# Token-major sums for the output projection and the second MLP matrix, gates as broadcast rows

## The chip, the cores and the metric

The kernel runs on one core of a Trainium2 chip. The metric is the device time of one execution in microseconds (us). TensorE (PE) multiplies, VectorE (DVE), ScalarE (ACT) and GpSimd (POOL) do the elementwise work, and SyncE (SP) issues all DMAs from one queue, in order.

## The reference, cut to what matters

Two layers act on 512 tokens of width 1024: 256 context tokens (`z`) and 256 latent tokens (`x`). Layer 1, the last, keeps the latent tokens alone behind its mixers.

```python
for l in range(DEPTH):                    # DEPTH = 2
    y = merged @ w_out                    # 1024 x 1024, end of the token mixers
    x = post_norm(x, mx[2] * y, ln1_g, ln1_b)
    m = square(relu(modulate(x, mx[3], mx[4]) @ w_mlp1)) @ w_mlp2   # 1024 -> 4096 -> 1024
    x = post_norm(x, mx[5] * m, ln2_g, ln2_b)
def post_norm(r, u, g, b): return layernorm(DN_ALPHA * r + u) * g + b
```

The same holds for `z` with its own gates `mz`. A gate has one value for each of the 1024 features, and one set for each half of the tokens.

## The kernel before, in words

All products are made in float32r, three matmuls for one: `W` loads a block of weights (512 KB, tile `raw`, three buffers), and `wsplit` splits it in four parts into `wh` (a cast on ACT, L191) and `wl` (the rest, a subtraction on DVE, L121). `mm3` then runs `wh`·`xh`, `wh`·`xl` and `wl`·`xh` for each of eight blocks of 128 input features (L216, L220, L221). A block of weights is 1024 input features by 128 output features, so the sums come out feature-major: 128 features on the partitions, 256 or 512 tokens along the row.

`out_proj` goes through its tokens in halves of 256 (`a`, called pair `pr` in the norms: two tiles `t` of 128 tokens). For each half it runs eight blocks of `w_out`, and ACT scales each sum by its gate column into a tile `mg` (called `uT`). `mlp` goes through the 4096 hidden features in quarters `q`. In a quarter, eight blocks of `w_mlp1` make the hidden tiles (`p`), and eight blocks of `w_mlp2` make partial sums that DVE adds up in eight tiles `mg` (called `acc`). The last quarter runs its `w_mlp2` blocks once for each half of the tokens, and DVE also scales them by the gate.

After every four blocks `done` starts `norm_seg`, which brings them into token-major form: `post_half` transposes four 128 x 128 pieces on PE into a PSUM bank (`gr` or `ch`), DVE adds `ALPHA` times the residual (`b`, L130), and `bn_stats` takes the row statistics. At the end of layer 1 PE does the addition too: it multiplies the residual by `ALPHA` times the identity (`kaid`, L477) and adds four products with the identity (`kmisc`, L479). When both halves of the features are there, `post_norm` normalizes on DVE, stores the result (`xd`), and `ln_T` transposes the next operand `hh`, `hl`.

What order the engines follow is set in two steps: `stream` and `pump` interleave the generators by a modelled clock (`COL`, `MM`), and a scheduler with a priority list then orders each engine's queue. Beside layer 0's output projection and MLP runs `feed` (`ada_sum`), which computes later gate columns on DVE (tiles `v` and `t`) from weights that take the same three `raw` buffers; `ada` does other columns on PE between the two stages. `small`, the mixers and `branch` lie ahead of all this.

Of the kernel before, what the change touches and what calls it, by code (L numbers as in the profile page):

```python
# [16 lines left out]
L = 512  # L17
# [70 lines left out]
class Net:  # L88
# [68 lines left out]
    def consts2(self):  # L157
        nc, K = self.nc, self.K
        mb = self.T("kmiscb", (128, 3, 128), BF16)
        nc.sync.dma_start(mb, K['miscb'])  # L160
        self.identb = mb[:, 0, :]
        self.negm = [mb[:, 1, :], mb[:, 2, :]]
        mk = self.T("kmmask", (128, 6, 128), BF16)
        nc.sync.dma_start(mk, K['mmask'])
        self.mmask = mk
        self.aident = self.T("kaid", (128, 128))
        self.ts(self.aident, self.ident, ALPHA)
        zrow = self.T("p", (128, 512))
        nc.gpsimd.memset(zrow, 0.0)
        self.imgs = []  # L170
        for j in range(2):
            im = self.dr.tile([4, 129, 128], F32, name=f"img{j}", tag=f"img{j}", bufs=1)
            nc.sync.dma_start(im[:, 0:128, :].rearrange("u p i -> p u i"), zrow.rearrange("p (u i) -> p u i", u=4))
            self.imgs.append(im)
        self.img_n = 0
# [280 lines left out]
                    self.stt(hl[k][:, c], ps[:, kk, :], s, tm, op0=ALU.mult, op1=ALU.subtract)  # L456
            yield 2 * self.MM, 0.3

    def post_begin(self, resid, g, b, tiles):
        nc = self.nc  # L460
        self.gbt = []
        for a in (g, b):
            t = self.T("b", (128, 1024))
            nc.sync.dma_start(t, a.partition_broadcast(128))
            self.gbt.append(t)
        self.res = {t: resid(t) for t in tiles}
        self.pn = {}

    def post_half(self, uT, t, hf, last):

        rh = self.res[t][:, hf * 512:(hf + 1) * 512]
        if not hf:
            self.pn[t] = [], self.T("pst", (128, 2, 6), bufs=4)
        pss, st = self.pn[t]
        ps = self.PS("gr" if t % 2 else "ch")
        if last:
            self.nc.tensor.matmul(ps, self.aident, rh, start=True, stop=False, skip_group_check=True)  # L477
            for k in range(4):
                self.nc.tensor.matmul(ps[:, k * 128:(k + 1) * 128], uT[hf * 4 + k][:, t * 128:(t + 1) * 128],  # L479
                                      self.ident, start=False, stop=(k == 3), skip_group_check=True)  # L480
        else:
            for k in range(4):
                self.tp(ps[:, k * 128:(k + 1) * 128], uT[hf * 4 + k][:, t * 128:(t + 1) * 128])
            self.stt(rh, rh, ALPHA, ps)
            ps = rh
        self.nc.vector.bn_stats(st[:, hf, :], ps)
        pss.append(ps)

    def post_norm(self, ts, out, last=False):

# [32 lines left out]
                self.tt(sm[t][:, 2:3], sm[t][:, 0:1], rs2[t])  # L523
                self.act(r, r, AF.Identity, scale=rs2[t], bias=sm[t][:, 2:3])

    def norm_seg(self, uT, pr, hf, out, last=False):

        for t in (2 * pr, 2 * pr + 1):
            self.post_half(uT, t, hf, last)
            yield (8 if last else 2) * self.MM, 0.5  # L530
        if hf:
            self.post_norm((2 * pr, 2 * pr + 1), out, last)
            if not last:
                yield 0.0, self.D_LN
                yield from self.ln_T(self.res, pr)


    def small_cols(self, l):
# [718 lines left out]
    def seg(mc, f, a):  # L1257

        w = 1 - a // 256
        return mc[:, f, w:w + 1]  # L1260

    def out_proj(self, l, done):
        t0 = self.t0
        mh, ml = [], []
        for k in range(8):
            hi = self.T("p", dt=F32R)
            lo = self.T("p", dt=F32R)
            self.act(hi[:, t0:], self.mg[k], AF.Copy, scale=0.5)
            self.stt(lo[:, t0:], self.mg[k], 0.5, hi[:, t0:].bitcast(F32), op0=ALU.mult, op1=ALU.subtract)
            mh.append(hi)  # L1270
            ml.append(lo)
        uT = []
        for a in range(t0, L, 256):
            for f in range(8):
                ps = yield from self.projg(self.I['w_out'][l][:, f * 128:(f + 1) * 128], (mh, ml), a, a + 256)
                if a == t0:
                    uT.append(self.T("mg"))
                self.act(uT[f][:, a:a + 256], ps, AF.Identity, scale=self.seg(self.modc[l, 2], f, a))
                if f % 4 == 3:
                    done(a // 256, f // 4, uT)  # L1280

    def mlp(self, l, begin, done):
        t0 = self.t0
        acc = [None] * 8
        for q in range(4):
            ah, al = [], []
            for j in range(8):
                c0 = q * 1024 + j * 128
                ps = yield from self.projg(self.I['w_mlp1'][l][:, c0:c0 + 128], self.h, t0)
                r = self.T("s1")  # L1290
                self.act(r[:, t0:], ps, AF.Relu)
                self.tt(r[:, t0:], r[:, t0:], r[:, t0:])
                hi = self.T("p", dt=F32R)
                lo = self.T("p", dt=F32R)
                self.nc.scalar.copy(hi[:, t0:], r[:, t0:])
                self.tt(lo[:, t0:], r[:, t0:], hi[:, t0:].bitcast(F32), op=ALU.subtract)
                ah.append(hi)
                al.append(lo)
            wp = lambda f: self.I['w_mlp2'][l][q * 1024:(q + 1) * 1024, f * 128:(f + 1) * 128]
            for f in range(8 if q < 3 else 0):  # L1300
                ps = yield from self.projg(wp(f), (ah, al), t0)
                if q == 0:
                    acc[f] = self.T("mg")
                    self.nc.scalar.copy(acc[f][:, t0:], ps)
                else:
                    self.tt(acc[f][:, t0:], ps, acc[f][:, t0:], op=ALU.add)
        begin()
        for a in range(t0, L, 256):
            for f in range(8):
                ps = yield from self.projg(wp(f), (ah, al), a, a + 256)  # L1310
                v = acc[f][:, a:a + 256]
                self.tt(v, ps, v, op=ALU.add)
                self.ts(v, v, self.seg(self.modc[l, 5], f, a))
                if f % 4 == 3:
                    done(a // 256, f // 4, acc)


    def run(self):
# [27 lines left out]
        for l in range(DEPTH):  # L1346
            last = l == DEPTH - 1
            segs = [1] if last else [0, 1]
            tiles = [t for pr in segs for t in (2 * pr, 2 * pr + 1)]
            self.t0 = 256 if last else 0  # L1350
            self.delays = self.DELAYS[l]
            self.early = 3
            sm = self.start(self.small(l, self.small_proj(l)), 1.0)
            self.mg = [None] * 8
            self.yd = {(b, k): self.dr.tile([128, 512], F32, name=f"yd{l}_{b}_{k}", tag=f"yd{b}_{k}", bufs=1)
                       for b in range(3) for k in range(8)}
            self.mixers(l, sm)
            self.drain(self.bg)
            self.post_begin(spilled(2 * l - 1) if l else load, I['ln1_g'][l], I['ln1_b'][l], tiles)
# [3 lines left out]
            self.stream(self.out_proj(l, lambda pr, hf, uT: self.start(self.norm_seg(uT, pr, hf, xd[2 * l]), 0.5)))  # L1363
# [9 lines left out]
            def begin():  # L1373
                if not last:
                    self.drain(self.bg)
                    self.ln_begin(l + 1, 0, 1)
                self.post_begin(spilled(2 * l), I['ln2_g'][l], I['ln2_b'][l], tiles)

            def done(pr, hf, acc):
                self.start(self.norm_seg(acc, pr, hf, self.out[0] if last else xd[2 * l + 1], last), 0.5)  # L1380
            self.stream(self.mlp(l, begin, done))
# [77 lines left out]
```

## Time and profile before

| | us |
|---|---|
| median of 3 runs | 2586.37 |
| lowest and highest run | 2582.62, 2587.11 |
| the profiled execution, its own time | 2590.78 |
| its span in the trace | 2589.0 |
| TensorE busy in it | 2504.6 |

The profiled execution is 4.4 us above the median of the runs. Times inside the trace count from the start of the span. Layer 0's output projection lies at about 1102 to 1166, its MLP from there to 1566, layer 1's output projection at 2333 to 2370, and its MLP from 2390 to the end.

### The profile page before, as it was taken

Reading aid. Unit: us, or ns where it says so; the run is one execution under the profiler, and the core shown is the slowest. Engines: PE = TensorE matmul, PEld = TensorE weight load, DVE = VectorE, ACT = ScalarE, POOL = GpSimd, SP = SyncE. Lnnn points to the kernel's source line nnn. Section 1 sums busy time; section 2 is a strip of 40 time slices with the busy share of each in tenths; the row PEclk is TensorE's granted clock in tenths of the full one; section 3 lists DMA queues with packets and bytes.
Section 4 is the critical chain, followed back from the end, with each engine's and each line's share of the span. In section 5 each row is a group of like instructions: output and inputs, shape, how many; then the busy total and the mean of one; then the engine's idle time right before and its main releaser. Section 6 shows DMA issues by size and latency. Waiting matters only on the chain.

```text
span 2589.0 us, 42418 instructions
## 1 busy us (share of the span) xinstructions
PE 2504.6 (97%) x15225; PEld 2153.7 (83%) x15225; DVE 1808.8 (70%) x4779; ACT 1223.0 (47%) x3608; POOL 179.3 (7%) x334
## 2 busy tenths in 40 slices
PE   7999999999999999989999998899999999999998
PEld 3788888888887888887888886788888888997998
DVE  4967767676678565687556477787777777776766
ACT  3544544554454233355333245455545555555653
POOL 1010010010110000000000001001101101000000
PEclk9999999999999999999999999899999999999999
DMA  7323323312325555466455444433343334676664
GB/s 233 94 83 91 103 78 91 95 54 75 93 62 172 158 156 166 129 190 211 143 166 153 125 139 118 115 106 107 84 122 93 84 94 119 190 213 201 199 189 128
DMA packets 538022, 337.91 MB, mean 131 GB/s; under 512 B 46816, under 2 KB 502098, under 8 KB 537810
## 3 DMA queue, kind: packets, MB, share of 16 engines
q1 hardware_dynamic: 537810, 335.19, 44.7%
q8 instruction: 120, 1.97, 0.3%
q14 instruction: 92, 0.75, 0.1%
HBM read 314.17 MB, written 20.97 MB: 129 GB/s over the span
## 4 chain that ended last, share of the span: by engine, by line
PE 78%; DVE 10%; DMA 5%; ACT 3%; issue 2%; POOL 1%; SPq 0%; DVEq 0%; ACTq 0%; POOLq 0%
PE psmm L216 19%; PE psmm L220 19%; PE psmm L221 18%; PE psmm L136 6%; PE psch L136 5%; PE pstr L136 4%; PE psgr L136 2%; DVE wl L121 2%; DVE p L130 2%; PE pstr L133 2%; PE psgr L1202 1%; DVE b L130 1%; DMA my<-img 1%; ACT wh L191 1%; DMA raw<-in_w_mlp_dram 1%
## 5 line engine op out<-in xcount | busy, mean ns | idle before, releaser
L191 ACT CAST wh<-raw 128x256 fp32r<-128x256 f32 x1736 | 609.6, 405 | 785.5 <-PE psmm L220 550.3
L121 DVE TENSOR_TENSOR wl<-raw,wh 128x256 fp32r<-128x256 f32 x1736 | 682.0, 429 | 221.4 <-ACT wh L191 218.4
L216 PE MATMUL psmm<-hh,wh 128*128 128x512 f32 (+1 forms) x2088 | 763.2, 366 | 11.3 <-ACT wh L191 5.2
L220 PE MATMUL psmm<-hl,wh 128*128 128x512 f32 (+1 forms) x2088 | 732.2, 351 | 1.6 <-POOL hl L121 1.6
L221 PE MATMUL psmm<-hh,wl 128*128 128x512 f32 (+1 forms) x2088 | 728.7, 350 | 3.4 <-DVE wl L121 3.4
L216 PEld LDWEIGHTS psmm<-hh,wh 128*128 128x128 f32 x2088 | 397.5, 191 | 62.3 <-ACT wh L191 7.5
L221 PEld LDWEIGHTS psmm<-hh,wl 128*128 128x128 f32 x2088 | 397.0, 190 | 57.6 <-DVE wl L121 5.5
L220 PEld LDWEIGHTS psmm<-hl,wh 128*128 128x128 f32 x2088 | 397.2, 190 | 48.0 <-POOL hl L121 2.8
L216 PE MATMUL psmm<-p,wh 128*128 128x256 f32 (+1 forms) x1152 | 374.8, 326 | 2.1 <-DVE mg L121 1.9
L221 PE MATMUL psmm<-p,wl 128*128 128x256 f32 (+1 forms) x1152 | 369.2, 321 | 4.7 <-DVE wl L121 4.6
L220 PE MATMUL psmm<-p,wh 128*128 128x256 f32 (+1 forms) x1152 | 367.9, 320 | 1.3 <-DVE p L130 1.1
L221 PEld LDWEIGHTS psmm<-p,wl 128*128 128x128 f32 x1152 | 218.1, 189 | 22.4 <-DVE wl L121 6.3
L216 PEld LDWEIGHTS psmm<-p,wh 128*128 128x128 f32 x1152 | 218.2, 190 | 17.4 <-ACT sm L116 1.5
L220 PEld LDWEIGHTS psmm<-p,wh 128*128 128x128 f32 x1152 | 218.2, 189 | 16.7 <-DVE p L130 1.6
L136 PE MATMUL psmm<-wh,hh 128*128 128x256 f32 x512 | 143.6, 280 | 0.0
L130 DVE SCALAR_TENSOR_TENSOR p<-ci,cw,p 128x512 f32<-128x512 f32 (+1 forms) x192 | 137.6, 721 | 8.3 <-ACT p L116 8.1
L136 PE MATMUL psmm<-wl,hh 128*128 128x256 f32 x512 | 143.4, 280 | 0.0
L136 PE MATMUL psmm<-wh,hl 128*128 128x256 f32 x512 | 143.2, 280 | 0.0
L136 PEld LDWEIGHTS pstr<-v,v 128*128 128x128 f32 x768 | 98.4, 191 | 11.4 <-issue 3.0
L136 PE MATMUL pstr<-v,v 128*128 128x128 f32 x768 | 103.3, 277 | 1.3 <-DVE hrs L125 0.4
L130 DVE SCALAR_TENSOR_TENSOR v<-raw,c,v 128x512 f32<-128x512 f32 x112 | 83.7, 747 | 21.9 <-DMA raw<-in_w_ada_dram 21.2
L136 PEld LDWEIGHTS psmm<-wl,hh 128*128 128x128 f32 x512 | 96.2, 188 | 0.7
(264 smaller groups left out, 3365.1 us busy)
## 6 DMA issues: line engine op xcount, KB each, us to landing
raw<-in_w_in_dram SPq DMA_DIRECT2D x224, 512.0 KB
raw<-in_w_mlp_dram SPq DMA_DIRECT2D x136, 512.0 KB
raw<-in_w_ada_dram SPq DMA_DIRECT2D x80, 512.0 KB
raw<-in_w_branch_dram SPq DMA_DIRECT2D x48, 512.0 KB
raw<-in_w_out_dram SPq DMA_DIRECT2D x24, 512.0 KB
p<-in_w_ada_dram SPq DMA_DIRECT2D x32, 256.0 KB
s<-const_toep_dram SPq DMA_DIRECT2D x40, 192.0 KB
yd<-s SPq DMA_DIRECT2D x24, 256.0 KB
```

What stands on the lines that cost most here:

```text
L121: (eng or self.nc.vector).tensor_tensor(out, a, b, op=op)
L130: self.nc.vector.scalar_tensor_tensor(out, a, s, b, op0=op0, op1=op1)
L133: self.nc.tensor.transpose(out, in_, ident if ident is not None else self.ident)
L136: self.nc.tensor.matmul(out, lhsT, rhs, start=start, stop=stop)
L191: self.nc.scalar.copy(hi, src)
L216: i = self.nc.tensor.matmul(ps, hi[:, k, :], a, start=(k == 0 and clear), stop=False, skip_group_check=not clear)
L220: self.nc.tensor.matmul(ps, hi[:, k, :], b, start=False, stop=False, skip_group_check=not clear)
L221: self.nc.tensor.matmul(ps, lo[:, k, :], a, start=False, stop=(k == 7), skip_group_check=not clear)
L1202: self.nc.tensor.matmul(O[i // 2][:, i % 2, :], W[:, cs(i)], V[:, j, :], start=(j == 0 and i % 2 == 0), stop=(j == (1 if i < 2 else 3)), s ...
```

## The change

`tokproj` swaps the operands: 128 tokens of the activations are the stationary operand, and 512 columns of the weights move. The sums come out token-major (128 tokens by 512 features, one PSUM bank), and no transpose is needed in front of the norm. A block of weights is now 256 input features by 512 output features, again 512 KB, and it is split in two parts. In layer 0 the three first quarters of the MLP keep four banks at once, and their sums are added into `acc` as before, by tile and half of the features. In layer 1 the four banks (`gr` and `ch`) hold the sums over all four quarters.

Since features lie along the row, the gate can't be a column any more. `post_begin` writes the gate columns to DRAM as rows (`gd`) and reads each half back as a row of 512, broadcast over 128 partitions (tiles `my` and `ci`). `post_half` multiplies the sum by it, adds the residual and takes the statistics. In layer 0's last quarter the sums so far are multiplied by the gate and added to the residual while the first MLP matrix runs.

```diff
-    def post_half(self, uT, t, hf, last):
+        self.gr = {}
+        for pr in sorted({t // 2 for t in tiles}):
+            d = self.dr.tile([8, 128], F32, name=f"gd{l}_{sec}_{pr}", tag=f"gd{l}_{sec}_{pr}", bufs=1)
+            nc.sync.dma_start(d.rearrange("k p -> p k"), self.modc[l, sec][:, :, 1 - pr])
+            for hf in range(2):
+                t = self.T("ci" if pr else "my", (128, 512))
+                nc.sync.dma_start(t, d[4 * hf:4 * hf + 4].rearrange("k p -> (k p)").partition_broadcast(128))
+                self.gr[pr, hf] = t
+
+    def post_half(self, ps, t, hf, acc=None):
...
-        ps = self.PS("gr" if t % 2 else "ch")
-        if last:
-            self.nc.tensor.matmul(ps, self.aident, rh, start=True, stop=False, skip_group_check=True)
-            for k in range(4):
-                self.nc.tensor.matmul(ps[:, k * 128:(k + 1) * 128], uT[hf * 4 + k][:, t * 128:(t + 1) * 128],
-                                      self.ident, start=False, stop=(k == 3), skip_group_check=True)
+        tm = self.T("s1")
+        self.tt(tm, ps, self.gr[t // 2, hf])
+        if acc is None:
+            self.stt(rh, rh, ALPHA, tm)
         else:
-            for k in range(4):
-                self.tp(ps[:, k * 128:(k + 1) * 128], uT[hf * 4 + k][:, t * 128:(t + 1) * 128])
-            self.stt(rh, rh, ALPHA, ps)
...
+            self.tt(rh, acc, tm, op=ALU.add)
+    def tokproj(self, ap, xs, order, pss, first=True, last=True):
+        xh, xl = xs
+        n = len(order) // 2
+        for k0 in range(0, 8, 2):
+            hi, lo = self.W(ap[k0 * 128:(k0 + 2) * 128, :], 2)
+            if k0 < 6:
+                todo = [(k, t) for k in range(2) for t in order[n:] + order[:n]]
+            else:
+                todo = [(k, t) for t in order for k in range(2)]
+            for kk, t in todo:
+                k = k0 + kk
+                c = slice(t * 128, t * 128 + 128)
+                self.mm(pss[t], xh[k][:, c], hi[:, kk, :], start=(first and k == 0), stop=False)
+                self.mm(pss[t], xl[k][:, c], hi[:, kk, :], start=False, stop=False)
+                self.mm(pss[t], xh[k][:, c], lo[:, kk, :], start=False, stop=(last and k == 7))
...
-                ps = yield from self.projg(self.I['w_out'][l][:, f * 128:(f + 1) * 128], (mh, ml), a, a + 256)
...
-                self.act(uT[f][:, a:a + 256], ps, AF.Identity, scale=self.seg(self.modc[l, 2], f, a))
+                pss = {t: self.PS("gr" if hf else "mm") for t in ts}
+                yield from self.tokproj(self.I['w_out'][l][:, hf * 512:(hf + 1) * 512], (mh, ml), ts, pss)
+                for t in ts:
+                    self.post_half(pss[t], t, hf)
```

PE's queue at the end of layer 1. Before, these rows follow the last three of 24 matmuls of a block (`psmm`): for each of the two tiles of tokens one product of the residual `b` and four of the sums `mg`.

```order
L216 MATMUL psmm_28105<-p_27792,wh_28095 128x256
L220 MATMUL psmm_28105<-p_27793,wh_28095 128x256
L221 MATMUL psmm_28105<-p_27792,wl_28096 128x256
L477 MATMUL psch_28132<-b_27800,kaid_276 128x512
L479 MATMUL psch_28132<-kmisc_63,mg_26013 128x128
L479 MATMUL psch_28132<-kmisc_63,mg_26052 128x128
L479 MATMUL psch_28132<-kmisc_63,mg_26091 128x128
L479 MATMUL psch_28132<-kmisc_63,mg_26130 128x128
L477 MATMUL psgr_28139<-b_27802,kaid_276 128x512
```

In the change the queue ends with the last block of `w_mlp2` itself, six matmuls for one tile of tokens and six for the other.

```order
L136 MATMUL psch_25058<-wh_26682,p_26482 128x512
L136 MATMUL psch_25058<-wh_26682,p_26483 128x512
L136 MATMUL psch_25058<-wl_26683,p_26482 128x512
L136 MATMUL psch_25058<-wh_26682,p_26526 128x512
L136 MATMUL psch_25058<-wh_26682,p_26527 128x512
L136 MATMUL psch_25058<-wl_26683,p_26526 128x512
L136 MATMUL psch_25059<-wh_26682,p_26482 128x512
L136 MATMUL psch_25059<-wh_26682,p_26483 128x512
L136 MATMUL psch_25059<-wl_26683,p_26482 128x512
```

The products with `kaid` and `kmisc` are gone, and the first tile's bank is complete six matmuls ahead of the second's.

DVE's queue in layer 0's output projection, around the first `post_half` of a pair. Before: `wl` are the splits, `v` and `t` the feed's sums, `b` the residual with a transposed bank added.

```order
L121 TENSOR_TENSOR wl_11014<-raw_11011,wh_11013 128x256 x4
L130 SCALAR_TENSOR_TENSOR v_10857<-raw_11027,c_10_84,v_10857 128x512
L130 SCALAR_TENSOR_TENSOR t_10858<-raw_11027,c_10_84,t_10858 128x512
L130 SCALAR_TENSOR_TENSOR v_10857<-raw_11027,c_10_84,v_10857 128x512
L130 SCALAR_TENSOR_TENSOR b_10780<-b_10780,psch_11035 128x512
L130 SCALAR_TENSOR_TENSOR t_10858<-raw_11027,c_10_84,t_10858 128x512
L486 BN_STATS pst_11034<-b_10780 128x6
L130 SCALAR_TENSOR_TENSOR b_10782<-b_10782,psgr_11049 128x512
L121 TENSOR_TENSOR wl_11075<-raw_11072,wh_11074 128x256
L486 BN_STATS pst_11048<-b_10782 128x6
L121 TENSOR_TENSOR wl_11075<-raw_11072,wh_11074 128x256 x3
```

In the change, at the same place:

```order
L121 TENSOR_TENSOR wl_10962<-raw_10959,wh_10961 128x512 x2
L121 TENSOR_TENSOR s_2085_10948<-psmm_10848,my_10788 128x512
L130 SCALAR_TENSOR_TENSOR v_10864<-raw_10970,c_10_84,v_10864 128x512
L130 SCALAR_TENSOR_TENSOR b_10778<-b_10778,s_2085_10948 128x512
L121 TENSOR_TENSOR s_2087_10953<-psmm_10849,my_10788 128x512
L488 BN_STATS pst_10947<-b_10778 128x6
L130 SCALAR_TENSOR_TENSOR b_10780<-b_10780,s_2087_10953 128x512
L130 SCALAR_TENSOR_TENSOR t_10865<-raw_10970,c_10_84,t_10865 128x512
L488 BN_STATS pst_10952<-b_10780 128x6
L121 TENSOR_TENSOR wl_10986<-raw_10983,wh_10985 128x512 x2
```

Two multiplications by the gate (`s` out of `psmm` and `my`) are new, and both splits of the next block (`wl_10986`) stand behind the whole group.

SP's queue early in layer 0's MLP in the change; ahead of the change the loads of `ada` and `mlp` weights followed one another here.

```order
L341 DMA t_11830<-in_b_ada_dram 4x128
L470 DMA gd_5_0_13721<-mc_5_2069_10861 128x8x1
L470 DMA gd_5_1_13727<-mc_5_2069_10861 128x8x1
L345 DMA raw_11834<-in_w_ada_dram 128x2x512
L473 DMA my_13723<-gd_5_0_13721 128x512
L196 DMA raw_11854<-in_w_mlp_dram 128x8x128
L345 DMA raw_11884<-in_w_ada_dram 128x2x512
L473 DMA my_13725<-gd_5_0_13721 128x512
```

The two writes `gd` wait for the gate columns `mc`, and the reads into `my` for the write; weight loads stand behind each.

## Rows read from the trace of the kernel before

**Rows 1.** The page: busy us of each engine, its share of the span, instructions.
```profile
PE 2504.6 (97%) x15225; PEld 2153.7 (83%) x15225; DVE 1808.8 (70%) x4779; ACT 1223.0 (47%) x3608; POOL 179.3 (7%) x334
```

**Rows 2.** Windows: busy us (instructions) of engines by stretch, clock, DMA share, GB/s.
```profile
1102.00:1166.00 64.00, 56.26 (x434) 52.89 (x433) 57.02 (x123) 33.32 (x88) 6.46 (x9) 0.95 0.63 193
...
1510.00:1566.00 56.00, 52.52 (x431) 50.37 (x429) 48.02 (x124) 28.98 (x77) 7.40 (x8) 1.00 0.51 154
...
2400.00:2576.00 176.00, 175.84 (x1494) 175.15 (x1493) 119.65 (x337) 100.93 (x310) 0.00 (x0) 1.00 0.63 179
```

**Rows 3.** Waits of PE, 1095 to 1170: us in total, times, longest.
```profile
PE psmm L221 <- DVE wl L121: 4.1, 3, 3.1
PE psch L133 <- ACT mg L116: 2.7, 4, 1.4
```

**Rows 4.** Timeline and chain (1170.33): last matmul of a stage, the norm's later steps.
```profile
1165.59 0.28 PE L221 MATMUL psmm<-p,wl 128*128 128x256 f32 x1
...
1170.33 1.33 DVE b L130 x2
...
1565.76 0.28 PE L221 MATMUL psmm<-p,wl 128*128 128x256 f32 x1
...
1570.20 1.41 DVE L130 SCALAR_TENSOR_TENSOR b<-b,sm,b 128x512 f32<-128x512 f32 x2
...
2369.18 0.28 PE L221 MATMUL psmm<-p,wl 128*128 128x256 f32 x1
...
2373.09 1.40 DVE L130 SCALAR_TENSOR_TENSOR b<-b,sm,b 128x512 f32<-128x512 f32 x2
...
2576.20 0.28 PE L221 MATMUL psmm<-p,wl 128*128 128x256 f32 x1
...
2584.22 1.28 DVE L130 SCALAR_TENSOR_TENSOR b<-b,sm,b 128x1024 f32<-128x1024 f32 x1
```

**Rows 5.** Timeline of PE (start, us), layer 1's MLP: 66 matmuls of 256 apart.
```profile
2419.74 0.28 PE L220 MATMUL psmm<-p,wh 128*128 128x256 f32 x1
...
2427.51 0.28 PE L220 MATMUL psmm<-p,wh 128*128 128x256 f32 x1
```

**Rows 6.** Timeline of PE, layer 0's MLP: 30 matmuls of 512 apart.
```profile
1299.62 0.39 PE L221 MATMUL psmm<-hh,wl 128*128 128x512 f32 x1
...
1306.62 0.39 PE L221 MATMUL psmm<-hh,wl 128*128 128x512 f32 x1
```

**Rows 7.** The page's groups: a stationary load (busy us, mean ns).
```profile
L220 PEld LDWEIGHTS psmm<-p,wh 128*128 128x128 f32 x1152 | 218.2, 189 | 16.7 <-DVE p L130 1.6 <-DVE p L121 0.6
```

**Rows 8.** The chain that ended last: transposes in layer 0's last quarter.
```profile
1523.75 0.44 PE psgr L133 x4
```

**Rows 9.** The same chain: additions on PE, end of layer 1.
```profile
2563.23 0.90 PE psch L479 x8
2564.84 0.86 PE psgr L477 x2
```

**Rows 10.** Waits of PE, 1500 to 1570.
```profile
PE psmm L216 <- DVE mg L121: 1.9, 3, 1.2
```

**Rows 11.** The chain: DVE's four splits; two sums, two statistics and their ends.
```profile
1120.37 1.34 DVE wl L121 x4
...
1167.55 1.28 DVE b L130 x2
1168.83 1.20 DVE pst L486 x2
1170.03 0.12 DVE sm L497
...
1170.17 0.15 DVE sm L125
```

**Rows 12.** The chain behind layer 0's output projection.
```profile
1176.10 6.14 DMA xd<-b
```

**Rows 13.** Waits of SP for small writes to DRAM, whole span.
```profile
SPq L831 <- DMA img<-vi: 15.5, 13, 1.9
```

More of the change, by code (lines that the diff above doesn't have):

```diff
@@ L165, in consts2 @@
         self.mmask = mk
-        self.aident = self.T("kaid", (128, 128))
-        self.ts(self.aident, self.ident, ALPHA)
         zrow = self.T("p", (128, 512))
@@ L457, in ln_T, with post_begin @@
             yield 2 * self.MM, 0.3
-    def post_begin(self, resid, g, b, tiles):
+    def post_begin(self, resid, g, b, tiles, l, sec):
         nc = self.nc
@@ L474, in post_half @@
         pss, st = self.pn[t]
-        ps = self.PS("gr" if t % 2 else "ch")
-        if last:
-            self.nc.tensor.matmul(ps, self.aident, rh, start=True, stop=False, skip_group_check=True)
-            for k in range(4):
-                self.nc.tensor.matmul(ps[:, k * 128:(k + 1) * 128], uT[hf * 4 + k][:, t * 128:(t + 1) * 128],
-                                      self.ident, start=False, stop=(k == 3), skip_group_check=True)
-        else:
-            for k in range(4):
-                self.tp(ps[:, k * 128:(k + 1) * 128], uT[hf * 4 + k][:, t * 128:(t + 1) * 128])
-            self.stt(rh, rh, ALPHA, ps)
-            ps = rh
-        self.nc.vector.bn_stats(st[:, hf, :], ps)
-        pss.append(ps)
+        tm = self.T("s1")
+        self.tt(tm, ps, self.gr[t // 2, hf])
+        if acc is None:
+            self.stt(rh, rh, ALPHA, tm)
+        else:
+            self.tt(rh, acc, tm, op=ALU.add)
+        self.nc.vector.bn_stats(st[:, hf, :], rh)
+        pss.append(rh)
     def post_norm(self, ts, out, last=False):
@@ L524, in post_norm, with norm_seg @@
                 self.act(r, r, AF.Identity, scale=rs2[t], bias=sm[t][:, 2:3])
[L526 to L535, printed above, removed]
+    def norm_seg(self, pr, out, last=False):
+        self.post_norm((2 * pr, 2 * pr + 1), out, last)
+        if not last:
+            yield 0.0, self.D_LN
+            yield from self.ln_T(self.res, pr)
     def small_cols(self, l):
@@ L1260, in seg @@
         return mc[:, f, w:w + 1]
+    def tokproj(self, ap, xs, order, pss, first=True, last=True):
[13 more added lines that the diff above has]
+                self.mm(pss[t], xh[k][:, c], lo[:, kk, :], start=False, stop=(last and k == 7))
+                yield 3 * 512 * self.COL
     def out_proj(self, l, done):
@@ L1271, in out_proj, with mlp @@
             ml.append(lo)
-        uT = []
-        for a in range(t0, L, 256):
-            for f in range(8):
-                ps = yield from self.projg(self.I['w_out'][l][:, f * 128:(f + 1) * 128], (mh, ml), a, a + 256)
-                if a == t0:
-                    uT.append(self.T("mg"))
-                self.act(uT[f][:, a:a + 256], ps, AF.Identity, scale=self.seg(self.modc[l, 2], f, a))
-                if f % 4 == 3:
-                    done(a // 256, f // 4, uT)
-    def mlp(self, l, begin, done):
+        for pr in range(t0 // 256, 2):
+            for hf in range(2):
+                ts = [2 * pr, 2 * pr + 1]
+                pss = {t: self.PS("gr" if hf else "mm") for t in ts}
+                yield from self.tokproj(self.I['w_out'][l][:, hf * 512:(hf + 1) * 512], (mh, ml), ts, pss)
+                for t in ts:
+                    self.post_half(pss[t], t, hf)
+                if hf:
+                    done(pr)
+    def mlp(self, l, begin, begin2, done):
         t0 = self.t0
-        acc = [None] * 8
+        acc, sums = {}, {}
+        wp = lambda q, hf: self.I['w_mlp2'][l][q * 1024:(q + 1) * 1024, hf * 512:(hf + 1) * 512]
         for q in range(4):
+            if q == 3:
+                begin()
             ah, al = [], []
@@ L1298, in mlp @@
                 al.append(lo)
[L1299 to L1315, printed above, removed]
+                if q == 3 and not t0:
+                    t, hf = j // 2, j % 2
+                    self.tt(acc[t, hf], acc[t, hf], self.gr[t // 2, hf])
+                    self.stt(acc[t, hf], self.res[t][:, hf * 512:(hf + 1) * 512], ALPHA, acc[t, hf])
@@ new lines, in mlp @@
+            if t0:
+                if q == 3:
+                    begin2()
+                for hf in range(2):
+                    if not q:
+                        sums[hf] = {t: self.PS("ch" if hf else "gr") for t in (2, 3)}
+                    yield from self.tokproj(wp(q, hf), (ah, al), [2, 3], sums[hf], q == 0, q == 3)
+                    if q == 3:
+                        for t in (2, 3):
+                            self.post_half(sums[hf][t], t, hf)
+                continue
+            if q == 3:
+                break
@@ new lines, in mlp @@
+            for hf in range(2):
+                pss = {t: self.PS("mm") for t in (0, 1)}
+                pss.update({t: self.PS("ch" if hf else "gr") for t in (2, 3)})
+                yield from self.tokproj(wp(q, hf), (ah, al), [0, 1, 2, 3], pss)
+                for t in range(4):
+                    if q == 0:
+                        acc[t, hf] = self.T("mg")
+                        self.nc.scalar.copy(acc[t, hf], pss[t])
+                    else:
+                        self.tt(acc[t, hf], pss[t], acc[t, hf], op=ALU.add)
@@ L1318, in run @@
+        if t0:
+            done(1)
+            return
+        begin2()
+        for pr in range(2):
+            for hf in range(2):
+                ts = [2 * pr, 2 * pr + 1]
+                pss = {t: self.PS("gr" if hf else "mm") for t in ts}
+                yield from self.tokproj(wp(3, hf), (ah, al), ts, pss)
+                for t in ts:
+                    self.post_half(pss[t], t, hf, acc[t, hf])
+            done(pr)
     def run(self):
@@ L1358, in run @@
             self.drain(self.bg)
-            self.post_begin(spilled(2 * l - 1) if l else load, I['ln1_g'][l], I['ln1_b'][l], tiles)
+            self.post_begin(spilled(2 * l - 1) if l else load, I['ln1_g'][l], I['ln1_b'][l], tiles, l, 2)
             self.ln_begin(l, 3, 4)
@@ L1362, in run @@
                 self.bg = self.start(self.feed(self.FEED, self.GAP[1]))
-            self.stream(self.out_proj(l, lambda pr, hf, uT: self.start(self.norm_seg(uT, pr, hf, xd[2 * l]), 0.5)))
+            self.stream(self.out_proj(l, lambda pr: self.start(self.norm_seg(pr, xd[2 * l]), 0.5)))
             self.hold = True
@@ L1373, in begin, with begin2 @@
             def begin():
+                self.post_begin(spilled(2 * l), I['ln2_g'][l], I['ln2_b'][l], tiles, l, 5)
+            def begin2():
                 if not last:
@@ L1376, in begin, with done @@
                     self.ln_begin(l + 1, 0, 1)
[L1377 to L1381, printed above, removed]
+            def done(pr):
+                self.start(self.norm_seg(pr, self.out[0] if last else xd[2 * l + 1], last), 0.5)
+            self.stream(self.mlp(l, begin, begin2, done))
             self.drain_all()
```

## The prediction

> **What bounds the kernel now.** I read the page first: TensorE is busy 97% of the span [rows 1], so the first question is whether the change takes work from PE. Then the stages it touches, by windows [rows 2]. Layer 1's MLP (2400 to 2576) is PE and nothing else: 175.84 of 176.00 us busy, DVE 119.65. Layer 0's last quarter and its `w_mlp2` blocks (1510 to 1566) are nearly so, 52.52 of 56.00, with DVE at 48.02. Layer 0's output projection (1102 to 1166) is another case: DVE is busy 57.02 of 64.00 us, PE 56.26, and the granted clock is 0.95. What PE waits for there is DVE's splits, 4.1 us, and ACT's scaled sums, 2.7 us [rows 3]. So what a removed matmul is worth differs: all of it in layer 1's MLP, little in layer 0's output projection. Last I read the joints, where PE has finished a stage and the norm runs on DVE before the next operand exists [rows 4]; there every us counts, whichever engine it is on.
>
> **The products themselves.** 1728 matmuls of 256 columns become 864 of 512: 384 in layer 0's output projection, 384 in its last quarter, 192 in layer 1's output projection, 768 in its MLP. From start to start, 66 matmuls of 256 take 7.77 us, 117.7 ns each [rows 5], and 30 of 512 take 7.00 us, 233.3 each [rows 6]. Two narrow ones cost 235.4, one wide one 233.3, so a pair saves 2.1 ns. In the three stages where PE is the bound that is 672 pairs, **1.4 us**. A stationary load lasts 189 ns [rows 7] and a narrow matmul starts every 117.7, so loads already run beside matmuls and halving their number frees no time. The bounds are 0 and 1.8 (864 pairs).
>
> The Trainium skill (TensorE: Matmul & The Clock Gate, section Back-to-back issue gap) says otherwise: in a stream of load and matmul the spacing is set by both, about 81 ns at 128 columns and 131 at 512. On a straight line between these 256 columns would take 98, and 864 pairs would save 864 x (2 x 98 - 131), about 56 us, an estimate from that page. The rows at 233.3 ns for 512 speak against it.
>
> **Transposes and additions on PE.** Gone are 32 transposes in each stage of layer 0, 16 in layer 1's output projection, and, at the end of layer 1, four additions of the residual with four products each. A transpose is 0.44/4 = 0.11 us [rows 8]; an addition is 0.86, its products 0.90 [rows 9]. The last two tiles of a stage belong to the joint; the others stand in PE's queue among matmuls. Layer 0's MLP: 24 x 0.11 = 2.6. Layer 1's output projection: 8 x 0.11 = 0.9. Layer 1's MLP: 2 x (0.86 + 0.90) = 3.5. Together **7.0 us**. Bounds: 4.4 if layer 0's part hides behind DVE, 7.0.
>
> **A bank that was late.** Before the end of layer 0's MLP PE waits 1.9 us for DVE to empty a bank `mm` [rows 10], as each block of 256 needs one of two. Now `mm` and `gr` alternate by half of the features, and a bank has four blocks, 48 matmuls or 11 us, to be emptied. I count **1.9 us**, bounds 0 and 1.9.
>
> **The joints.** Before, the last matmul ends, DVE or ACT scales the sum, PE transposes, DVE adds and takes statistics, and two operations form (r - mean) x g. From the last matmul's end (start + 0.28) to the end of these two: 1171.66 - 1165.87 = 5.8, 1571.61 - 1566.04 = 5.6, 2374.49 - 2369.46 = 5.0 [rows 4]. Now the first tile's bank is full six matmuls (1.4 us) early, so its gate and addition are done when the second tile ends. Behind that DVE does, in its order: gate 0.64 (half of the pair of 1.28, the nearest row for a 512 operation), statistics 0.60, addition 0.64, 0.12, statistics 0.60, 0.15, the two operations 1.33 [rows 4, 11]: 4.1 us. That saves 1.7, 1.5 and 1.0. At layer 1's end DVE finishes 2585.50 - 2576.48 = 9.0 behind the last matmul; now 4.1 + 0.12 + 1.28 + 0.15 + 1.33 + 1.28 = 8.2, so 0.8. Together **5.0 us**. Bounds: 0.8, if the first three vanish because the chain goes on through the store of the residual, 6.14 us [rows 12], and 5.0.
>
> **Layer 0's output projection.** DVE gets eight gates, 8 x 0.64 = 5.1 us; the splits get 16 x (1.34 - 1.28) = 1.0 cheaper [rows 11]. That is +4.1 on an engine busy 57 of 64 us. Against it stand ACT's wait, 2.7 [rows 3], and the transposes, 24 x 0.11 = 2.6, which PE no longer has. Upward the bound is +4.1. Downward: the 434 matmuls of the window [rows 2] at 117.7 ns are 51 us, so -13. I take **0**, nearer to DVE's row, since DVE is the engine that is full.
>
> **What is hidden.** Six writes of gates and twelve reads join SP's queue. A read waits for its write; such waits are 15.5/13 = 1.2 us, the longest 1.9 [rows 13]. Behind it stand weight loads, and behind these the splits. In layer 0 a block feeds PE for 24 x 0.2333 = 5.6 us and three are loaded ahead, so I count nothing; without that cover it is 6 x 1.9 = 11.4. In layer 0's last quarter DVE prepares `acc` with 16 operations, 10.2 us, while the first matrix keeps PE busy for 8 x 5.6 = 45 us with DVE mostly idle. In layer 1 the sums stay in their banks, which takes some 24 additions from an engine that had room: nothing.
>
> **Sum.** 1.4 + 7.0 + 1.9 + 5.0 + 0 = 15.3. The profiled execution took 2590.8, so 2575.5; it lies 4.4 above the median of 2586.4, which becomes **2571**. About 0.2% (5.2 us) is what a measurement can tell from no change here.
>
> **Rivals.**
> - *The forecast*, 0.60; its own range 2564 to 2578.
> - *Output projection set free*, 0.14: with ACT's scaling and PE's transposes gone, PE no longer waits there, and half of the 13 us comes back: 2571 - 6.5, about 2564. For it: the waits and the clock at 0.95 [rows 2, 3]. Against: DVE's load rises.
> - *Gains absorbed*, 0.13: the first three joints (4.2) are lost to the store, layer 0's transposes (2.6) and the bank's wait (1.9) to DVE, and DVE's 4.1 shows in the output projection. 15.3 - 12.8 = 2.5 is left: 2584, no change.
> - *DVE's queue blocks*, 0.11, the slower side: a gate waits for PE's bank, and the splits of the next block stand behind it. The group is 0.64 x 4 + 0.60 x 2 = 3.8 us, with two feed sums 5.1, and only one block (12 x 0.2333 = 2.8 us) is split ahead in the output projection. Before, a group stood there too, without the gates. If PE loses the whole 5.1 at all eight places in layer 0, that is +41 - 15: 2612. It turns slower than before by 0.2% from 20.5/8 = 2.6 us a place.
> - *Wider is faster*, 0.02: if a wide matmul came at the pace of its load, 189 ns, 864 x (235.4 - 189) = 40 us more would go, some 2531. The rows at 233.3 contradict it. The section of the Trainium skill named above is a rule of this kind.
>
> Faster is the first, second and last: 0.76; same 0.13; slower 0.11. The range reaches from the second case with its bound, 2557, to the third, 2584.
>
> **What would show it.** The 512 matmuls in layer 1's MLP start 233 ns apart. No transposes precede the norms, and PE's wait for `mg` is gone. Behind the last matmul of a stage the two operations end after 4.1 us, and after 8.2 at the end. Layer 0's output projection still takes about 64 us with DVE near 0.9. It is wrong if PE waits longer for splits beside the gates, if weights come late behind the gate rows, or if wide matmuls are slower with weights as the moving operand.

## The result and the profile after: 17 us slower

| | before | after |
|---|---|---|
| median us (5 runs each) | 2585.83 | 2604.82 |
| lowest and highest | 2582.62, 2587.11 | 2596.37, 2611.04 |
| ratio, 95% interval | | 1.0066 [1.0051, 1.0081] |
| the profiled execution: own time, span | 2590.78, 2589.0 | 2604.82, 2603.0 |

The ratio's 0.66% of 2586 is 17 us slower (the two medians lie 19.0 apart), where 15 us faster was forecast. The page after says first that the work did shrink. It shows busy us, share and instructions of each engine, and then the chain that ended last by engine:

```profile
PE 2497.8 (96%) x14241; PEld 2104.8 (81%) x14241; DVE 1797.1 (69%) x4566; ACT 1195.0 (46%) x3384; POOL 180.7 (7%) x334
...
PE 77%; DVE 9%; DMA 7%; ACT 3%; issue 3%; POOL 1%; SPq 0%; DVEq 0%; ACTq 0%; POOLq 0%
```

PE has 984 fewer instructions and 7 us less busy time than in [rows 1], in a span that is 14 us longer. The chain's share of DMA is the new thing. In the chain's pieces (start, us, what) one finds which transfers:

```profile
916.81 11.21 DMA gd<-mc
...
1206.57 11.52 DMA gd<-mc
...
1610.42 9.71 DMA raw<-in_w_in_dram
...
2406.41 13.60 DMA raw<-in_w_mlp_dram
...
2434.59 11.19 PE psgr L136 x48
```

Four places, and each is a write of gate columns or the weight load behind one (the third and fourth write are issued at 1605.7 and 2404.7). The first:

DMA traffic from 914 to 934 in slices of 0.5 us: busy share of the DMA engines in tenths, GB/s, and the packets.

```profile
DMA  9999966487000000454235435232276999896968
GB/s 348 336 365 385 262 176 266 35 24 7 0 0 0 0 0 0 52 73 31 22 29 33 22 13 24 23 29 37 59 72 170 365 395 287 299 242 193 254 217 262
DMA packets 4298, 2.70 MB, mean 135 GB/s; under 512 B 2219, under 2 KB 3247, under 8 KB 4297
```

Two writes of 4 KB are issued at 916.8 and 917.2. Their 4-byte packets are gone by 919. Then nothing at all moves for 3 us, and until 928.5 the queue brings 13 to 73 GB/s instead of some 300. SP waits for the write too, as its next instruction reads it:

```profile
SPq L473 <- DMA gd<-mc: 17.6, 2, 9.4
```

But the load of 512 KB issued ahead of that wait, at 917.9, comes no faster than this either, so it looks as if every transfer were held up; e4, which has no read, parts the two. What that does to the engines is best seen in layer 1's MLP, behind the write at 2404.7. Waits of ACT and of PE from 2395 to 2440 (total us, times, longest):

```profile
ACT wh L189 <- DMA raw<-in_w_mlp_dram: 12.0, 4, 9.6
```
```profile
PE psmm L214 <- ACT s L116: 6.6, 1, 6.6
```

The casts wait for weights, and the matmuls for ACT, because the activation that empties their bank stands behind those casts in ACT's queue. The stage, from its first product to the end of its last, as a window (busy us and counts of PE, PEld, DVE, ACT, POOL, then clock, DMA share, GB/s):

```profile
2398.84:2591.18 192.34, 184.77 (x1159) 165.95 (x1157) 115.66 (x269) 102.94 (x268) 1.58 (x2) 0.97 0.62 176
```

Before, the same stage took 185.9 us:

```profile
2390.56:2576.48 185.92, 185.48 (x1564) 183.67 (x1563) 127.09 (x357) 110.12 (x339) 1.58 (x2) 1.00 0.63 180
```

The other large loss lies ahead of the changed stages: layer 0's first `w_out` load is issued at 1080.51 instead of 1073.05, 7.5 us late, after the stop at 917. In e1, which has no such stop there, it is issued at 1072.99.

```profile
1080.51 0.37 SPq L196 DMA_DIRECT2D raw<-in_w_out_dram  x1
```

### The profile page after: what moved, and what is told of

Its sections match the earlier page's. It is cut to its first block, busy times and chain, and to the rows that moved or that the text cites. A ratio compares the mean times of both kernels' runs of the same rounds, so it can differ in the third digit from the quotient of the medians.

```text
span 2603.0 us, 40009 instructions
## 1 busy us (share of the span) xinstructions
PE 2497.8 (96%) x14241; PEld 2104.8 (81%) x14241; DVE 1797.1 (69%) x4566; ACT 1195.0 (46%) x3384; POOL 180.7 (7%) x334
## 4 chain that ended last, share of the span: by engine, by line
PE 77%; DVE 9%; DMA 7%; ACT 3%; issue 3%; POOL 1%; SPq 0%; DVEq 0%; ACTq 0%; POOLq 0%
PE psmm L214 15%; PE psmm L218 14%; PE psmm L219 14%; PE psmm L136 10%; PE psch L136 8%; PE psgr L136 7%; PE pstr L136 4%; DVE p L130 2%; DVE wl L121 2%; PE pstr L133 2%; DMA raw<-in_w_ada_dram 1%; DMA raw<-in_w_mlp_dram 1%; PE psgr L1200 1%; DMA gd<-mc 1%; ACT wh L189 1%
## 5 line engine op out<-in xcount | busy, mean ns | idle before, releaser
L189 ACT CAST wh<-raw 128x256 fp32r<-128x256 f32 (+1 forms) x1544 | 588.3, 432 | 812.4 <-PE psmm L218 426.7
L121 DVE TENSOR_TENSOR wl<-raw,wh 128x256 fp32r<-128x256 f32 (+1 forms) x1544 | 663.1, 463 | 274.5 <-ACT wh L189 271.7
L214 PE MATMUL psmm<-p,wh 128*128 128x512 f32 (+1 forms) x384 | 134.6, 351 | 3.5 <-DVE s L130 3.5
L218 PE MATMUL psmm<-p,wh 128*128 128x512 f32 (+1 forms) x384 | 131.9, 344 | 1.1 <-DVE p L130 1.1
L219 PE MATMUL psmm<-p,wl 128*128 128x512 f32 (+1 forms) x384 | 131.1, 341 | 0.0
L136 PE MATMUL psgr<-wh,p 128*128 128x512 f32 x384 | 121.8, 401 | 1.4 <-ACT wh L189 1.4
L136 PE MATMUL psmm<-wh,p 128*128 128x512 f32 x352 | 111.3, 399 | 0.5 <-ACT s L116 0.3
L136 PEld LDWEIGHTS psmm<-wh,hh 128*128 128x128 f32 x512 | 96.2, 188 | 0.7
```

The costliest lines, as they stand in the source:

```text
L121: (eng or self.nc.vector).tensor_tensor(out, a, b, op=op)
L136: self.nc.tensor.matmul(out, lhsT, rhs, start=start, stop=stop)
L189: self.nc.scalar.copy(hi, src)
L214: i = self.nc.tensor.matmul(ps, hi[:, k, :], a, start=(k == 0 and clear), stop=False, skip_group_check=not clear)
L218: self.nc.tensor.matmul(ps, hi[:, k, :], b, start=False, stop=False, skip_group_check=not clear)
L219: self.nc.tensor.matmul(ps, lo[:, k, :], a, start=False, stop=(k == 7), skip_group_check=not clear)
```

## The experiments

Three theories. **A**: the write of 4-byte elements stops all transfers. **B**: only SP's order is at fault (a read waits for the write, loads stand behind the read). **C**: the loss is elsewhere, in the gates on DVE or in the order of work. Times are medians; ratios are against the kernel before on the same chip, whose medians were 2587.30 (first four runs), 2585.49 (next four) and 2586.72 (last three).

| run | us | ratio, 95% interval | mean clock of its runs |
|---|---|---|---|
| e1_rows_by_pe | 2581.14 | 0.9981 [0.9972, 0.9989] | 0.988 |
| e2_act_queue | 2606.47 | 1.0079 [1.0066, 1.0092] | 0.983 |
| e3_no_write | 2587.92 | 1.0004 [0.9995, 1.0013] | 0.986 |
| e4_before_plus_write | 2600.88 | 1.0059 [1.0045, 1.0074] | 0.988 |
| e5_ada_behind | 2581.86 | 0.9983 [0.9972, 0.9993] | 0.989 |
| e6_half_elements | 2609.62 | 1.0092 [1.0078, 1.0106] | 0.986 |
| e7_64_byte_elements | 2586.55 | 1.0004 [0.9994, 1.0013] | 0.991 |
| e8_layer1_only | 2581.10 | 0.9986 [0.9975, 0.9997] | 0.991 |
| e9_layer0_only | 2589.72 | 1.0012 [1.0003, 1.0021] | 0.989 |
| e10_old_outproj_l0 | 2586.46 | 0.9995 [0.9986, 1.0004] | 0.989 |
| e12_spread_elements | 2588.05 | 1.0007 [0.9997, 1.0017] | 0.990 |

**e1: the gate rows made on PE, and written as rows.**

```diff
-            nc.sync.dma_start(d.rearrange("k p -> p k"), self.modc[l, sec][:, :, 1 - pr])
+            pg = self.PS("tr")[:8, :128]
+            self.tp(pg, self.modc[l, sec][:, :, 1 - pr])
+            row = self.T("gw", (8, 128))
+            nc.scalar.copy(row, pg)
+            nc.sync.dma_start(d, row)
```

> The gate columns are transposed on PE (six transposes of 128 x 8), copied by ACT and written to DRAM as eight rows of 512 B instead of 1024 elements of 4 B; everything else is as in the change. In the trace of the change nothing moves on the DMA queue for 3 us behind each scattered write, and little for 6 more, at four places. Theory A (the scattered write stops all transfers) and theory B (only SP's order is at fault: a read waits for the write, weight loads stand behind the read) both say that most of the loss goes: 7 us ahead of layer 0's output projection and some 6 to 10 in layer 1's MLP, so about 2583 to 2590. Theory C (the loss is somewhere else: the gates on DVE, the order of `ada` among the matmuls) says 2600 to 2606.

2581.14: C falls, and the change without its scattered write beats the kernel before by 6 us. The write now also stands later in SP's order than in the change, so e1 alone does not part A from B.

**e2: the same writes and reads, issued by ACT.**

```diff
-            nc.sync.dma_start(d.rearrange("k p -> p k"), self.modc[l, sec][:, :, 1 - pr])
+            nc.scalar.dma_start(d.rearrange("k p -> p k"), self.modc[l, sec][:, :, 1 - pr])
-                nc.sync.dma_start(t, d[4 * hf:4 * hf + 4].rearrange("k p -> (k p)").partition_broadcast(128))
+                nc.scalar.dma_start(t, d[4 * hf:4 * hf + 4].rearrange("k p -> (k p)").partition_broadcast(128))
```

> As the change, but the six writes and twelve reads of the gate rows are issued by ACT instead of SP, so that no weight load stands behind them in SP's order. Theory B says that the loss goes: 2583 to 2590. Theory A says that weight loads still land some 10 us late behind each write, whoever issues it: 2597 to 2608. Theory C: 2600 to 2606.

2606.47. The time alone does not settle B, since ACT now stands behind the write in its own order (`s` waits 9.6 us for `gd` there). Traffic from 914 to 934 again:

```profile
DMA  9998952575000007636256552443567899999999
GB/s 360 373 414 328 266 193 96 7 6 5 0 0 0 0 1 25 105 42 26 15 35 22 17 28 20 32 19 26 33 92 96 221 255 212 198 340 389 397 393 414
```

The stop is the same from another issuer, and SP, which has no read behind a write any more, gets nothing either: B falls as the main cause, and e4 confirms it. The Trainium skill (DMA: Bandwidth & Descriptors, section Issuing engines are not separate DMA queues) says that DMAs run on the same engines whoever starts them; this run agrees.

**e3: no write; the reads take a row of `ln1_g`** (so the gates are left out of the result).

```diff
-            d = self.dr.tile([8, 128], F32, name=f"gd{l}_{sec}_{pr}", tag=f"gd{l}_{sec}_{pr}", bufs=1)
-            nc.sync.dma_start(d.rearrange("k p -> p k"), self.modc[l, sec][:, :, 1 - pr])
+            d = self.I['ln1_g'][l]
...
-                nc.sync.dma_start(t, d[4 * hf:4 * hf + 4].rearrange("k p -> (k p)").partition_broadcast(128))
+                nc.sync.dma_start(t, d[512 * hf:512 * hf + 512].partition_broadcast(128))
```

> As the change, but without the writes: the twelve broadcast reads stand where they stood and read a row of ln1_g in place of the gates. Theories A and B: 2580 to 2588, as nothing waits and nothing is stopped. Theory C: 2600 to 2606. What is left over the 2571 of the prediction is then the reads themselves and the order of work.

2587.92, 17 us under the change, but 7 over e1. It is no clean price of the reads: with no write to wait for, they were also issued earlier, two of them among the loads of the mixers. Its mean clock is 0.986 instead of 0.988; why it is 7 us slower than e1 stays open.

**e4: the kernel before, with the six writes alone.** Behind `self.pn = {}` in `post_begin`:

```diff
+        for pr in sorted({t // 2 for t in tiles}):
+            d = self.dr.tile([8, 128], F32, name=f"gd{l}_{sec}_{pr}", tag=f"gd{l}_{sec}_{pr}", bufs=1)
+            nc.sync.dma_start(d.rearrange("k p -> p k"), self.modc[l, sec][:, :, 1 - pr])
```

> The kernel before with only the six scattered writes of the gate columns added; no instruction reads what they write. Theory A: each of four places costs part of its 9 to 10 us, so 2586 plus 10 to 20, 2596 to 2606. Theory B: no read waits, so nothing is held up: 2584 to 2589. Theory C: 2584 to 2589.

2600.88, 13.6 us slower, with nothing that reads or waits. Traffic from 912 to 932 (writes at 914.6 and 915.0):

```profile
GB/s 393 397 385 213 201 229 29 6 7 4 0 0 0 0 0 8 102 36 27 16 29 19 24 27 30 15 19 19 33 51 37 241 326 397 374 356 347 336 221 49
```

A is shown: this write alone makes most of the loss of 17 to 19 us. With the 15.3 us that was forecast as gain it would nearly cancel; so the gain must be smaller too (e1, e5, e8, e9). Taken out of the change itself (e1), the write is worth more, 2604.8 - 2581.1 = 23.7 us, but there the write's place in SP's order moves with it.

**e6, e7, e12: what in the write does it.** In e4 the write becomes, in turn:

```diff
+            nc.sync.dma_start(d[0:4].rearrange("k p -> p k"), self.modc[l, sec][:, 0:4, 1 - pr])   # e6
+            nc.sync.dma_start(d, self.modc[l, sec].rearrange("p k w -> p (k w)"))                  # e7, d [128, 16]
+            nc.sync.dma_start(d[:, :, 0].rearrange("k p -> p k"), self.modc[l, sec][:, :, 1 - pr]) # e12, d [8, 128, 128]
```

> The kernel before with six scattered writes of 512 elements of 4 B each (1024 in the run that gave 2600.9). No instruction reads them. If the stop lasts by the element, the added 13.6 us halve: 2592 to 2596. If each write costs the same whatever its length: 2599 to 2603.

> The kernel before with six writes of the same gate columns as they lie, 128 elements of 64 B each (twice the bytes, an eighth of the elements). If the small elements are the cause, by their number: 2587 to 2591. If any write from many partitions into one small piece of DRAM stops the queue: 2597 to 2603.

> The kernel before with six scattered writes of 1024 elements of 4 B, each element 512 B from the next (before: side by side). Nothing reads them. If the stop comes from many small writes into the same few lines of DRAM: 2586 to 2592. If the size of an element is enough: 2597 to 2606.

Half the elements cost more, not less: 24 us, outside both forecasts. Needing half of a gate, these writes were mostly issued earlier, one pair at 1142.9 and 1144.9, in layer 0's output projection, which waits for weights. Traffic of e6 from 1143 to 1163:

```profile
GB/s 196 91 131 373 381 112 93 52 38 16 20 59 31 27 24 33 47 23 17 48 17 24 55 231 333 331 354 266 164 107 74 29 74 123 131 33 74 90 188 115
```

From 1146.5 to 1154.5, behind the first write alone, 16 to 59 GB/s come; the small packets of the second write show only from 1153 to 1157 (549 under 512 B). So 512 elements stop the queue for some 8 us, 1024 or 2048 at once for 10 (above): the length is not in proportion to the number of elements. That the price goes by the place is argued from this, not shown. Elements of 64 B cost nothing that can be told (+1 us), and neither do 1024 elements of 4 B that lie 512 B apart (+1.3). Traffic of e7 from 2397 to 2417, behind its write at 2398.9:

```profile
GB/s 175 300 341 259 91 15 1 0 4 94 113 302 350 321 326 336 323 265 351 321 57 43 74 207 344 327 95 238 300 361 204 170 275 296 190 297 199 333 204 68
```

Traffic of e12 from 2397 to 2417, behind its write at 2396.2:

```profile
GB/s 5 3 0 23 62 161 312 346 331 347 342 262 293 348 308 27 38 82 220 348 314 131 175 280 323 239 170 232 285 258 229 221 303 253 102 129 210 292 274 175
```

Behind both writes there is a gap, but of 2 to 3 us instead of 10. So it is not small elements as such, but many of them side by side in 2 to 4 KB of DRAM; what distance would be enough was not tried. The Trainium skill (DMA: Bandwidth & Descriptors, section Specifications) says that below 512 B a transfer is a read-modify-write. By that alone e12 would stop as e4 does; it does not, so the measurement adds that neighbours matter.

**e5: `ada` held behind layer 0's output projection.** In e1 and in the change PE waits 6.2 us, by the profile for `ada` weights, ahead of the last twelve products of the output projection, which I took to be ready (waits of PE after, 1095 to 1195):

```profile
PE psch L136 <- DMA raw<-in_w_ada_dram: 6.4, 2, 6.2
```
```diff
-                    self.mm(ps[0:2, :], self.c2[:, k, :], raw[:, k2, :], start=(k == 0), stop=(k == 7))
+                    with self.tc.issue_after(self.last_mm.ins) if after else nullcontext():
+                        self.mm(ps[0:2, :], self.c2[:, k, :], raw[:, k2, :], start=(k == 0), stop=(k == 7))
...
-                self.mm(pss[t], xh[k][:, c], lo[:, kk, :], start=False, stop=(last and k == 7))
+                self.last_mm = self.nc.tensor.matmul(pss[t], xh[k][:, c], lo[:, kk, :], start=False,
+                                                     stop=(last and k == 7))
```

The same edit also holds the `ada` products behind layer 0's MLP and layer 1's output projection.

> As the version whose gate rows PE transposes (2581.1), and the sixteen matmuls of `ada` at the end of layer 0's output projection are held behind its last matmul. In that version two of them stand among the last twelve, and PE waits 6.2 us there for `ada` weights while the twelve are ready. If this order is what the output projection lost: about 3 us less, 2576 to 2579. Rival: the `ada` weights and the first weights of the MLP, which come through the same three buffers, end that joint anyway: 2580 to 2583.

2581.86: no gain, and the time the rival gave. But the same window of e5 shows another cause than either: the twelve were not ready. PE's wait is now for DVE's splits, and DVE's queue there says why:

```profile
PE psgr L1281 <- DVE wl L121: 5.4, 3, 4.9
```
```profile
1159.00 1.27 DVE L121 TENSOR_TENSOR s<-psmm,ci 128x512 f32<-128x512 f32 x2
1160.19 1.28 DVE L130 SCALAR_TENSOR_TENSOR b<-b,s 128x512 f32<-128x512 f32 x2
1161.39 1.27 DVE L493 BATCH_NORM_STATS2 pst<-b 128x6 f32<-128x512 f32 x2
1162.59 1.27 DVE L121 TENSOR_TENSOR wl<-raw,wh 128x512 fp32r<-128x512 f32 x2
```

Two gates, two additions and two statistics, 3.6 us in all, stand ahead of the splits of the last block, and PE goes on at 1163.31. In e1 the same splits start at 1161.28, when PE has waited since 1157.4: most of its 6.2 us there hid this wait.

**e8, e9, e10: one layer, one stage.** The methods of before stand beside the new ones, and `run` picks by layer (e8: new in layer 1; e9: new in layer 0; e10: e8 with layer 0's MLP new as well). `ada` is held as in e5 behind the new stages alone.

```diff
+            new = l == 1                                   # e9: l == 0
...
+            if new:
                 self.stream(self.mlp(l, begin, begin2, done))
+            else:                                          # e10: without this branch
+                self.stream(self.mlp_old(l, begin_old, done_old))
```

> Layer 0 as before, layer 1 as in the version with transposed gate rows and `ada` held behind. From the traces of before and of that version, start to start: the lead is 0 at layer 1's mixers and 8 at the end, so layer 1 alone should give 2587 - 8 = 2579 (2577 to 2582), with the four additions and eight transposes less on PE as the cause. Rival: the lead in layer 1 came from the state in which layer 0 left the queues: 2584 to 2587.

> Layer 0 as in the version with transposed gate rows and `ada` held behind, layer 1 as before. By the terms of the prediction layer 0 is worth 0.8 + 2.6 + 1.9 + 1.7 + 1.5 = 8.5 us: 2577 to 2579. By the traces of the runs so far its MLP is 2 to 5 us shorter, its two joints are as long as before (they end with `ada` weights, not with the norm), and the mean granted clock is 0.988 instead of 0.991, so that 0 to 3 us are left: 2583 to 2587.

> Layer 0's output projection as before, everything else as in the version with transposed gate rows. If the wide form of that stage is what costs clock (17 and 10 us at half clock between 1100 and 1200 in two profiles of the wide form, 6.8 in both of the narrow one) and the MLP of layer 0 saves 3 us: 2577 to 2580, at a clock near 0.990. Rival: that stage is neutral, 2580 to 2583, clock 0.988.

By the medians layer 1 alone gives 4.4 us (inside its forecast), layer 0 alone loses 3.0 (outside both of its forecasts), and e10 comes out at 2586.46 with a clock of 0.989, above both of its forecasts. The two layers alone add up to a gain of 1.4; together (e5) they gave 3.6. With intervals of 2.3 to 2.8 us each way these cannot be told apart well.

## Why the prediction was wrong, step by step

**The step that failed: "What is hidden ... so I count nothing".** I took the price of a gate write from writes of another kind (1.2 us, [rows 13]) and asked only who waits for it. The write's own cost to all other transfers was not a question I put. The cover of "a block feeds PE for 5.6 us and three are loaded ahead" was reckoned for a wait of 2 us, not for 10 us in which little comes. My uncovered price, 11.4, was near the 13.6 of e4 by accident: its mechanism (six reads that each wait for their write) is not the one shown.

**The products: right.** 48 products of 512 take 11.19 us in the chain above, 233.1 ns each, against 233.3 from [rows 6]. The rival "wider is faster" fell. The section of the Trainium skill named there (TensorE: Matmul & The Clock Gate, Back-to-back issue gap) gives 131 ns; this case does not show it.

**Transposes and additions: a size was off.** I read 0.86 and 0.90 of [rows 9] as one addition and its products, but the rows are `x2` and `x8`: two additions and the products of two. So layer 1's term is 1.8, not 3.5. With the rate's 384 x 2.1 ns = 0.8 that makes 2.6; in e1, where no write stops, the stage took 183.2 us instead of 185.9, 2.7 less. Window of e1 from first to last product:

```profile
2386.24:2569.43 183.19, 182.19 (x1160) 163.51 (x1158) 115.02 (x268) 102.50 (x267) 1.57 (x2) 0.99 0.62 185
```

Layer 0's MLP, first to last product, took 390.6 us before (391.0 in e8, which has the old form too), 388.8 in e1, 385.6 in e5 and e9 and 385.8 in e10. 192 x 2.1 ns = 0.4, with 2.6 and 1.9 for the bank that was late, is 4.9, so this forecast was right: three of four profiles give 5. PE's wait for `mg` from 1500 to 1570 [rows 10] is gone in all of them.

**The joints: the chain was right, half of its worth was not there.** Behind the last matmul of layer 1's output projection (2378.95) the two operations end 4.0 us later in the change, as forecast (4.1). DVE's timeline after:

```profile
2381.51 0.14 DVE L125 TENSOR_SCALAR sm<-sm 128x1 f32<-128x1 f32 x1
2381.57 1.40 DVE L130 SCALAR_TENSOR_TENSOR b<-b,sm,b 128x512 f32<-128x512 f32 x2
```

But PE does not go on from there. It does `ada` and the first half of the tokens, and the first product behind the joint waits for weights, before and after alike. Before, and then after, at the end of layer 0's MLP:

```profile
1576.13 0.39 PE L216 MATMUL psmm<-hh,wh 128*128 128x256 f32 x1 [1.78 <-ACT wh L191]
```
```profile
1584.86 0.38 PE L214 MATMUL psmm<-hh,wh 128*128 128x256 f32 x1 [1.74 <-ACT wh L189]
```

From the end of the last product to this one it is 10.1 us before (1566.04 to 1576.13), 9.5 after (1575.37 to 1584.86) and 10.0 in e5, where 1.5 less was forecast. Behind layer 0's output projection it is 9.6 before and 9.1 in e5 (1.7 forecast), behind layer 1's 21.1 and 19.8 (1.0 forecast). From the last product to the end of the program it is 12.5 us before and 11.9 in e5, 0.6 where 0.8 was forecast. Together that is some 2.5 of 5.0.

**Layer 0's output projection: 0 held.** Its window after, from the first product to the last, answers to the first of [rows 2]:

```profile
1107.00:1178.00 71.00, 59.72 (x236) 42.77 (x237) 59.40 (x103) 27.35 (x51) 7.12 (x9) 0.90 0.57 178
```

In the change it begins 7.5 us late (1107.64 instead of 1100.18) and lasts 70.1 us instead of 65.7; part of that is two `ada` products and the wait ahead of them, as e1 has them too and lasts 68.4. In e5, without the scattered write and with `ada` held, it is nearly as long as before, 66.5: the first matmul of `ada` behind it starts at 1166.23 before and 1166.73 in e5, both with the first `w_out` load at 1073. DVE bounds it, as the row said. "Output projection set free" fell. "DVE's queue blocks", my slower side, took place once, not at eight places: in the change PE's waits for `wl` from 1095 to 1195 add up to 1.7 us, but e5 brings out one of 4.9 that the wait for `ada` had hidden. Before, the longest such wait was 3.1 [rows 3].

**What is left.** e1's span is 7.7 us shorter than that of before and its median 6.2, where 15.3 was forecast: 1.7 were counted double, some 2.5 of the joints were not there. Part of the rest may go to the clock: over the 79 runs of before made beside the experiments, a straight line through time and mean granted clock falls 12.4 us for 0.010 of clock (correlation -0.58, so it explains a third of their scatter), and layer 0's new form brings the mean from 0.9907 to 0.9885 (e9), 2.7 us by that line. By the same line, an estimate, some 7 of the change's 17 to 19 us go with its clock of 0.984. In e1's stretches of 10 us PE is less busy just ahead of where it falls (PE's busy time second, clock third from the right):

```profile
1150.00:1160.00 10.00, 6.70 (x29) 4.34 (x28) 10.00 (x18) 5.98 (x13) 3.18 (x3) 1.00 0.65 197
1160.00:1170.00 10.00, 6.46 (x14) 2.71 (x15) 7.65 (x13) 0.00 (x0) 0.00 (x0) 0.66 0.57 178
1170.00:1180.00 10.00, 7.70 (x23) 2.90 (x22) 8.78 (x22) 4.03 (x12) 2.64 (x3) 0.90 0.85 271
1180.00:1190.00 10.00, 9.85 (x61) 9.27 (x61) 7.34 (x16) 5.70 (x13) 1.49 (x3) 0.76 0.92 299
```

PE stood waiting, and the granted clock then went to its lower level (1.2 GHz) for a part of the next three stretches. But e10 speaks against this place as the cause. Its output projection is the old one, and its clock there is that of before (0.97 from 1100 to 1200, 0.91 in e1):

```profile
1100.00:1200.00 100.00, 87.02 (x628) 75.21 (x626) 81.16 (x177) 54.09 (x138) 12.53 (x17) 0.97 0.66 205
```

The mean over its runs is 0.9887 all the same, and it gains nothing. So where layer 0's new form loses clock is open, and that the clock is the cause of its missing gain is argued and not shown; no run held the clock. Why layer 0 alone is even 3 us slower stays open too: the profiled execution of e9 is its quickest (2584.64), and in it layer 0's MLP is 5 us shorter, as forecast.

## What to carry to other kernels

A small transfer is priced by what it does to the transfers around it, not only by who waits for it: before a column of 4-byte elements is written to DRAM, turn it (a transpose on PE, 0.11 us in [rows 8], and a copy) and write whole rows, as e1 does. A shorter chain at a joint is worth something only if the first instruction behind the joint waits for that chain; read its wait first. A wait that the profile puts down to one releaser can hide another that ended just before; move the first and see what is left, as e5 does. And read the count of a row before its time.

## What the runs showed that was not expected

- A DMA of 1024 elements of 4 B from 128 partitions into 4 KB of DRAM, side by side, stops the core's transfers: some 3 us of nothing or nearly nothing and some 6 at 10 to 105 GB/s in place of some 300, whether SP or ACT issues it; 512 elements in 2 KB hold them to 16 to 59 GB/s for 8 us. Elements of 64 B (+1 us for six writes), or the same elements 512 B apart (+1.3), leave a gap of 2 to 3 us that costs nothing that can be told.
- The stop of two such writes 0.4 us apart (918 to 928.5) is no longer than that of one (2406 to 2416.5).
- Runs of one kernel differ with the granted clock: the change's two quickest runs (2596.4, 2596.9) had a mean of 0.987 and 0.988, the other three (2604.8 to 2611.0) 0.982 to 0.983.
